# Gated recurrence: the scores of two levels in one stretch of TensorE tiles, with the odd level's queries copied aside by ScalarE

## The chip, the cores and the metric

One NeuronCore of a Trainium2 chip runs the whole program; nothing is shared with another core. The metric is the device time of one execution in microseconds, the median of several runs. The profile is one such execution, recorded by the hardware.

## The reference, cut to what matters

A two-layer encoder trunk is run on two batches (512 and 256 tokens, here 768 tokens side by side, width 1024). Layer 0 mixes tokens by a gated recurrence in both directions, layer 1 by windowed attention, and each layer has a feed-forward block ahead of its mixer and one behind. The change touches the recurrence alone:

```python
def gla_chunk_scan(q, k, v, logf):
    """q, k, logf: [B,T,H,K]; v: [B,T,H,V]. S_t = diag(f_t) S_{t-1} + k_t v_t^T, o_t = S_t^T q_t."""
    ...
        b = jnp.cumsum(fi.astype(F32), axis=1)
        o_inter = jnp.einsum('bchk,bhkv->bchv', qf * jnp.exp(b), S)
        ...
        A = jnp.einsum('bthk,btshk,bshk->bhts', qf, jnp.exp(rel), kf)
        o_intra = jnp.einsum('bhts,bshv->bthv', A, vf)
```

There are 8 heads of 128 channels. The scan runs once forward and once backward in time, and the two results are added.

## The kernel before, in words

**Where the recurrence stands.** The feed-forward block comes first. Then `hgrn` runs the heads one behind the other. For each head `hgrn_proj` makes queries, two forget gates and keys by projections (three matmuls in float32r for each product, lines 258 to 260), and `hgrn_scan` does the recurrence. While head h is scanned, the projection of head h+1 is fed in between in pieces: `weave` runs one step of the scan up to its `yield`, then some pieces of the projection, so that TensorE has work while VectorE and ScalarE prepare the next step. In head 3 the value projection of the second half is fed in as well (42 pieces in place of 18), in head 6 there are four pieces fewer, and in head 7 it is the projection of the output gate that is fed in.

**The levels.** Within a block of 128 tokens the scores are made by 7 levels of halving. At level l the tokens stand in runs of J = 2^l; a query of one run meets the keys of the run beside it. `q` and `k` hold, for both directions, values that are multiplied in place by the running products of gates (`totals`) after each level, so that they fit the next one. One level before is: ScalarE copies the keys of the level into `kop` in token order (line 702); TensorE makes the scores of 6 blocks in 12 matmuls of a 128x64 tile (`scan_scores`, line 675), reading the queries straight out of `q`; VectorE puts the result into the score matrix `A` (`put`: a copy at line 693 or a copy under a mask at line 696, two instructions a level); VectorE multiplies `q` (line 718, one instruction), `k` (line 722, one for each direction) and `totals` (line 724). At level 0 the scores of every token with itself are made as well, from the untouched queries `qs` and the sum of keys `kd`. Behind level 6 come the transposes (line 738), the chunk sums (line 746) and the output (line 770).

**What sets the order.** The program is written in this order, and a scheduler then lays out a fixed queue for each engine; an engine works through its queue in order, and waits between engines are semaphores. All three of TensorE, VectorE and ScalarE carry both the scan of head h and the projection of head h+1: on ScalarE the evictions of the projection (line 657), the weight casts (line 166) and the complement of the gates (line 662) stand between the key copies; on VectorE the weight remainders (line 167) and the gate arithmetic (lines 661, 663, 664) stand between the level's instructions.

Of the kernel before, what the change touches and what calls it, by code (L numbers as in the profile page):

```python
# [16 lines left out]
P = 128  # L17
# [5 lines left out]
T = TA + TB  # L23
# [3 lines left out]
LEVELS = 7  # L27
# [20 lines left out]
class Trunk:  # L48
# [559 lines left out]
            yield  # L608

    @staticmethod  # L610
    def weave(main, feed, pieces, steps=LEVELS + 1):
        used = 0
        for i, _ in enumerate(main):
            while used * steps < (i + 1) * pieces:
                used += 1
                next(feed, None)
# [53 lines left out]
    def scan_scores(self, lhs, rhs):  # L670
        ps = self.ps(NBLK * 64)
        for b in range(NBLK):
            for par in range(2):
                rows = slice(par * 64, (par + 1) * 64)
                self.nc.tensor.matmul(ps[rows, b * 64 : (b + 1) * 64], lhs(b)[:, rows], rhs(b, par), start=True, stop=True)  # L675
        return ps

    def hgrn_scan(self, hd, v):
        nc = self.nc
        h, qs, kd, f, q, k = (hd[n] for n in ("h", "qs", "kd", "f", "q", "k"))  # L680
        ka = self.big([P, 2, T])
        kop, A = ka[:, 0, :], ka[:, 1, :]
        totals = self.big([P, 2, T])
        blk = lambda t, b: t[:, b * P : (b + 1) * P]

        def put(level, ps):
            for par in range(2):
                rows = slice(par * 64, (par + 1) * 64)
                c = 1 - par if level == LEVELS - 1 else par
                dst = A.rearrange("p (b c j) -> p b c j", c=2, j=64)[rows, :, c, :]  # L690
                src = ps[rows, :].rearrange("p (b j) -> p b j", j=64)
                if level in (0, LEVELS - 1):
                    nc.vector.tensor_copy(dst, src)
                    continue
                m = self.masks[rows, level, c * 64 : (c + 1) * 64].unsqueeze(1).to_broadcast([64, NBLK, 64])
                nc.vector.copy_predicated(dst, m, src)

        tot, base = f, 0
        for l in range(LEVELS):
            c, J = T >> l, 1 << l  # L700
            kv = bass.AP(k.tensor, k.offset, [list(k.ap[0]), [2 * J, c // 2], [T + J, 2], [1, J]])
            nc.scalar.copy(kop.rearrange("p (b g j) -> p b g j", g=2, j=J), kv)

            def rhs(b, par):
                part = list(q.ap[0])
                if J == 64:
                    return bass.AP(q.tensor, q.offset + b * P + (0 if par else T + J), [part, [1, J]])
                at = q.offset + b * P + par * 64
                return bass.AP(q.tensor, at, [part, [2 * J, 64 // (2 * J)], [T + J, 2], [1, J]])

            put(l, self.scan_scores(lambda b: blk(kop, b), rhs))
            if l == 0:
                own = lambda b, par: qs[:, b * P + par * 64 : b * P + (par + 1) * 64]
                put(LEVELS, self.scan_scores(lambda b: blk(kd, b), own))
            part = [list(q.ap[0])]
            both = bass.AP(q.tensor, q.offset, part + [[T + J, 2], [2 * J, c // 2], [1, J]])
            t = bass.AP(tot.tensor, tot.offset + base + 1, [list(tot.ap[0]), [T - 1, 2], [2, c // 2], [0, J]])
            nc.vector.tensor_mul(both, both, t)
            for d in range(2):
                xv = self.halves(k, l, d, d)  # L720
                t = tot[:, 1 - d, base + 1 - d : base + c : 2].unsqueeze(2).to_broadcast([P, c // 2, J])
                nc.vector.tensor_mul(xv, xv, t)
            nbase = 0 if l == 0 else base + c
            nc.vector.tensor_mul(
                totals[:, :, nbase : nbase + c // 2], tot[:, :, base : base + c : 2], tot[:, :, base + 1 : base + c : 2]
            )
            tot, base = totals, nbase
            yield

        F, Bk = 1, 0  # L730
        order = ((0, 0), (0, 1), (0, 2), (0, 4), (1, 1), (1, 2), (1, 3), (1, 5))
        kT = self.big([P, 8, P])
        S = self.big([P, 8, P])
        for half in range(2):
            pt = self.ps()
            for i in range(4):
                d, b = order[half * 4 + i]
                nc.tensor.transpose(pt[:, i * P : (i + 1) * P], blk(k[:, d, :], b), self.ident)
            nc.scalar.copy(kT[:, half * 4 : half * 4 + 4, :], pt.rearrange("p (a b) -> p a b", a=4))
        vb = lambda b: v[b][:, h * P : (h + 1) * P]  # L740
        pds = []
        for half in range(2):
            pd = self.ps()
            for i in range(4):
                d, b = order[half * 4 + i]
                nc.tensor.matmul(pd[:, i * P : (i + 1) * P], kT[:, half * 4 + i, :], vb(b), start=True, stop=True)  # L746
            pds.append(pd)
        state = {}
        for d, steps in ((0, ((0, None), (1, 0), (2, 1), (4, None))), (1, ((3, None), (2, 3), (1, 2), (5, None)))):
            for b, prev in steps:  # L750
                i = order.index((d, b))
                ds = pds[d][:, (i % 4) * P : (i % 4 + 1) * P]
                if prev is None:
                    nc.scalar.copy(S[:, i, :], ds)
                else:
                    dec = totals[:, 1 - d, base + b : base + b + 1]
                    nc.vector.scalar_tensor_tensor(S[:, i, :], S[:, order.index((d, prev)), :], dec, ds, ALU.mult, ALU.add)
                state[(d, b)] = S[:, i, :]
        yield
        pos = [self.ps(n) for _, n in SEQS]  # L760
        for b in range(NBLK):
            s, i = (0, b) if b < 4 else (1, b - 4)
            o = pos[s][:, i * P : (i + 1) * P]
            terms = [(blk(A, b), vb(b))]
            if (0, b - 1) in state and b != 4:
                terms.append((blk(q[:, F, :], b), state[(0, b - 1)]))
            if (1, b + 1) in state and b != 3:
                terms.append((blk(q[:, Bk, :], b), state[(1, b + 1)]))
            for j, (l_, r_) in enumerate(terms):
                nc.tensor.matmul(o, l_, r_, start=(j == 0), stop=(j == len(terms) - 1))  # L770
        for s, (off, n) in enumerate(SEQS):
            nb = n // P
            sq = self.tmp(n)
            nc.scalar.square(sq, pos[s])
            for b in range(nb):
                nc.scalar.copy(vb(off // P + b), pos[s][:, b * P : (b + 1) * P])
            nc.vector.tensor_reduce(
                self.hss[:, h, off // P : off // P + nb], sq.rearrange("p (b j) -> p b j", b=nb), AX.X, ALU.add
            )
# [485 lines left out]
```

## Time and profile before

| What | Value |
|---|---|
| Time, median of 3 runs | 2799.03 us (2798.24 to 2800.07) |
| The profiled execution | 2799.1 us, its span 2797.3 us, the 1.8 us beside it being start and end |
| Instructions in the span | 42176 |
| Granted TensorE clock | 0.998 of full speed |
| The scan, first to last score matmul | 580.1 us to 921.2 us, 1536 matmul records on line 675 |
| Key copies of ScalarE, line 702 | 56, median 837 ns |

In the profile a TensorE time is that of the start of an operation and its modelled end, so matmuls that follow each other overlap in the list; the distance from one start to the next is what an operation costs. A score matmul in float32 appears as two records. The score group of one level is therefore 24 records, and two groups behind each other are one stretch.

### The profile page before, as it was taken

How to read it: one execution, taken by the hardware profiler on the slowest of the kernel's cores; microseconds unless marked ns; L12 is line 12 of the kernel's file. 1: busy time of each engine (PE TensorE's matmuls, PEld its weight loads, DVE VectorE, ACT ScalarE, POOL GpSimd, SP SyncE). 2: the span in 40 equal slices, each digit the busy share in tenths (PEclk: the TensorE clock that was granted, in tenths of full speed). 3: DMA queues.
4: the chain of work that ended last, by engine and by line, in shares of the span. 5: the costliest groups of instructions: out<-in, count | busy, mean ns of one | idle time of the engine just before them, and what ended most of it. 6: DMA issues, size and time to landing. Idle time of an engine off the chain costs nothing.

```text
span 2797.3 us, 42176 instructions
## 1 busy us (share of the span) xinstructions
PE 2768.5 (99%) x16129; PEld 2493.3 (89%) x16129; DVE 2168.3 (78%) x3750; ACT 1283.9 (46%) x2383; POOL 308.6 (11%) x312
## 2 busy tenths in 40 slices
PE   8999999999999999999999999999999999999998
PEld 8999999888888889999999999999876679999998
DVE  7788788578598658788878878887847768788877
ACT  7444444434344435444445544444546655444443
POOL 1111111000000001211111121111100001211110
PEclk9999999999999999999999999999999999999999
DMA  5554564311111322655444255544512113655443
GB/s 160 132 125 117 125 140 124 113 52 41 54 39 31 103 72 76 143 132 128 119 113 124 76 145 132 122 117 118 143 61 76 46 47 76 146 135 121 125 111 108
DMA packets 330106, 291.47 MB, mean 104 GB/s; under 512 B 11608, under 2 KB 257840, under 8 KB 329904
## 3 DMA queue, kind: packets, MB, share of 16 engines
q1 hardware_dynamic: 294064, 212.43, 25.4%
q0 software_dynamic: 31680, 62.93, 13.3%
q10 hardware_dynamic: 4160, 13.42, 1.4%
q8 instruction: 126, 2.06, 0.3%
q14 instruction: 76, 0.62, 0.1%
HBM read 216.39 MB, written 9.44 MB: 81 GB/s over the span
## 4 chain that ended last, share of the span: by engine, by line
PE 94%; DVE 4%; ACT 1%; issue 0%; DMA 0%; DVEq 0%; SPq 0%; ACTq 0%
PE ps L418 40%; PE ps L482 20%; PE ps L258 9%; PE ps L259 8%; PE ps L260 8%; PE ps L675 2%; PE ps L1139 1%; PE ps L1089 1%; PE ps L770 1%; PE ps L1129 1%; PE ps L320 1%; PE ps L746 1%; DVE w L200 0%; DVE big L264 0%; DVE w L167 0%
## 5 line engine op out<-in xcount | busy, mean ns | idle before, releaser
L418 PE MATMUL ps<-big,w 128*128 128x384 f32 x6720 | 1172.6, 334 | 1.2 <-ACT tA L435 1.2
L418 PEld LDWEIGHTS ps<-big,w 128*128 128x128 f32 x6720 | 1165.3, 188 | 6.8 <-ACT tA L435 4.8
L199 ACT CAST w<-wr 128x512 fp32r<-128x512 f32 x600 | 415.8, 707 | 687.8 <-DVE wr L213 355.3
L200 DVE TENSOR_TENSOR w<-wr,w 128x512 fp32r<-128x512 f32 (+1 forms) x520 | 449.0, 867 | 181.3 <-ACT w L199 171.9
L482 PE MATMUL ps<-w,big 128*128 128x512 f32 x2520 | 575.7, 389 | 0.9 <-DVE x L504 0.9
L482 PEld LDWEIGHTS ps<-w,big 128*128 128x128 f32 x2520 | 472.6, 188 | 98.9 <-ACT big L263 1.3
L504 DVE SCALAR_TENSOR_TENSOR x<-ps,x 128x512 f32<-128x512 f32 x468 | 303.9, 681 | 10.7 <-PE ps L260 10.0
L141 POOL DMA_DIRECT2D s<-wr x120 | 105.1, 876 | 1706.0 <-DMA wr<-in_ffn_w_dram 847.1
L258 PE MATMUL ps<-w,big 128*128 128x512 f32 x624 | 253.0, 405 | 0.3
L260 PE MATMUL ps<-w,big 128*128 128x512 f32 x624 | 244.4, 392 | 1.0 <-DVE big L327 1.0
L259 PE MATMUL ps<-w,big 128*128 128x512 f32 x624 | 244.1, 391 | 0.0
L258 PE MATMUL ps<-big,w 128*128 128x384 f32 (+2 forms) x640 | 221.6, 348 | 2.7 <-ACT big L263 1.6
L259 PE MATMUL ps<-big,w 128*128 128x384 f32 (+2 forms) x640 | 217.0, 339 | 0.7 <-DVE big L264 0.6
L260 PE MATMUL ps<-big,w 128*128 128x384 f32 (+2 forms) x640 | 215.8, 337 | 0.0
L263 ACT CAST big<-tA 128x384 fp32r<-128x384 f32 x296 | 148.0, 513 | 144.7 <-DVE tA L450 64.9
L264 DVE TENSOR_TENSOR big<-tA,big 128x384 fp32r<-128x384 f32 x296 | 179.0, 615 | 13.2 <-ACT big L263 12.2
L167 DVE TENSOR_TENSOR w<-wr,w 128x1024 fp32r<-128x1024 f32 x92 | 112.0, 1220 | 69.3 <-ACT w L166 63.5
L166 ACT CAST w<-wr 128x1024 fp32r<-128x1024 f32 x92 | 96.7, 1052 | 120.6 <-PE ps L259 101.1
L258 PEld LDWEIGHTS ps<-w,big 128*128 128x128 f32 x624 | 117.2, 188 | 30.1 <-issue 6.8
L200 POOL TENSOR_TENSOR w<-wr,w 128x512 fp32r<-128x512 f32 x80 | 123.0, 1537 | 171.6 <-ACT w L199 170.2
L260 PEld LDWEIGHTS ps<-w,big 128*128 128x128 f32 x624 | 117.1, 188 | 27.1 <-DVE big L327 1.7
L259 PEld LDWEIGHTS ps<-w,big 128*128 128x128 f32 x624 | 117.4, 188 | 21.5 <-issue 0.4
(160 smaller groups left out, 2960.5 us busy)
## 6 DMA issues: line engine op xcount, KB each, us to landing
wr<-in_ffn_w_dram SPq DMA_DIRECT2D x264, 512.0 KB, 3.9
s<-in_ffn_w_dram SPq DMA_DIRECT2D x120, 256.0 KB, 3.1
s<-wr POOLq DMA_DIRECT2D x120, 256.0 KB, 4.4
wr<-wr POOLq DMA_DIRECT2D x80, 256.0 KB, 3.7
wr<-in_hg_w_in_dram SPq DMA_DIRECT2D x40, 512.0 KB, 3.8
wr<-wr POOLq DMA_DIRECT2D x20, 512.0 KB, 4.6
spill<-x ACTq DMA_DIRECT2D x12, 512.0 KB, 2.7
x<-spill ACTq DMA_DIRECT2D x12, 512.0 KB, 3.3
```

Source lines behind the costliest of these rows:

```text
L141: self.nc.gpsimd.dma_start(out, src, accum_op=ALU.add)
L167: self.nc.vector.tensor_sub(lo, raw, hi.bitcast(F32))
L199: nc.scalar.copy(h, src)
L200: low = (eng or nc.vector).tensor_sub(l, src, h.bitcast(F32)).ins
L258: nc.tensor.matmul(out, a[0], b[0], start=first, stop=False)
L259: nc.tensor.matmul(out, a[0], b[1], start=False, stop=False)
L260: nc.tensor.matmul(out, a[1], b[0], start=False, stop=last)
L263: self.nc.scalar.copy(hi, src)
L264: self.nc.vector.tensor_sub(lo, src, hi.bitcast(F32))
L418: self.nc.tensor.matmul(ps, a[x], b[y], start=first and k == 0 and i == 0, stop=k == 3 and i == 2, skip_group_check=True,)
L482: nc.tensor.matmul(ps, a[x], w[y], start=name == chain and kp == 0 and q == 0, stop=kp == 1 and q == 2, skip_group_check=True,)
L504: self.nc.vector.scalar_tensor_tensor(x, ps, c, x, ALU.mult, ALU.add)
```

## The change

Two levels now share one step of the scan. Step by step: level 0 with the scores of every token with itself, as before; levels 1 and 2; levels 3 and 4; levels 5 and 6. `yield` stands only behind the even levels, and `weave` divides the projection pieces by 5 steps in place of 8.

In a step with levels l-1 and l (l even), the operands of the odd level are copied aside when it is their turn, its in-place multiplications are done, then the operands of the even level are copied, and only then both score groups are issued: the even level first, the odd one pinned right behind it. The odd level's queries would be overwritten by then, so ScalarE copies them into `qs` in token order (line 707), 24 copies more in all. Its keys go to `spare`, the even level's keys to `kd`, whose first contents are no longer needed (line 705).

```diff
-    def weave(main, feed, pieces, steps=LEVELS + 1):
+    def weave(main, feed, pieces, steps=LEVELS // 2 + 2):
...
-                self.nc.tensor.matmul(ps[rows, b * 64 : (b + 1) * 64], lhs(b)[:, rows], rhs(b, par), start=True, stop=True)
-        return ps
+                mm = self.nc.tensor.matmul(
+                    ps[rows, b * 64 : (b + 1) * 64], lhs(b)[:, rows], rhs(b, par), start=True, stop=True
+                )
+        return ps, mm.ins
...
-        kop, A = ka[:, 0, :], ka[:, 1, :]
+        spare, A = ka[:, 0, :], ka[:, 1, :]
...
+        def operands(l):
+            J = 1 << l
+            part, runs = list(q.ap[0]), [[2 * J, T // (2 * J)], [T + J, 2], [1, J]]
+            kop = kd if l and l % 2 == 0 else spare
+            view = lambda t: t.rearrange("p (b g j) -> p b g j", g=2, j=J)
+            nc.scalar.copy(view(kop), bass.AP(k.tensor, k.offset, [list(k.ap[0])] + runs))
+            if l % 2:
+                nc.scalar.copy(view(qs), bass.AP(q.tensor, q.offset, [part] + runs))
+
+            def rhs(b, par):
+                at = b * P + par * 64
+                if l % 2:
+                    return qs[:, at : at + 64]
...
+            return l, lambda b: blk(kop, b), rhs
+
+        own = lambda b, par: qs[:, b * P + par * 64 : b * P + (par + 1) * 64]
+        waiting = []
         tot, base = f, 0
         for l in range(LEVELS):
             c, J = T >> l, 1 << l
-            kv = bass.AP(k.tensor, k.offset, [list(k.ap[0]), [2 * J, c // 2], [T + J, 2], [1, J]])
-            nc.scalar.copy(kop.rearrange("p (b g j) -> p b g j", g=2, j=J), kv)
...
-            put(l, self.scan_scores(lambda b: blk(kop, b), rhs))
+            waiting.append(operands(l))
             if l == 0:
-                own = lambda b, par: qs[:, b * P + par * 64 : b * P + (par + 1) * 64]
-                put(LEVELS, self.scan_scores(lambda b: blk(kd, b), own))
+                waiting.append((LEVELS, lambda b: blk(kd, b), own))
+            if l % 2 == 0:
+                banks, last = [], None
+                for level, left, right in reversed(waiting) if l else waiting:
+                    with self.tc.issue_after(last) if last else nullcontext():
+                        ps, last = self.scan_scores(left, right)
+                    banks.append((level, ps))
+                for level, ps in banks:
+                    put(level, ps)
+                waiting = []
...
             tot, base = totals, nbase
-            yield
+            if l % 2 == 0:
+                yield
```

**TensorE, head 1, levels 1 and 2.** In these rows `ps_5622` (before) and `ps_5625` (now) are the bank of a projection piece of head 2, `big_5123` is `q` of head 1, `big_5121` holds `qs` and `kd`, `big_5553` or `big_5556` holds the key copies. Before:

```order
L258 MATMUL ps_5622<-big_4591,w_5213 128x512
L259 MATMUL ps_5622<-big_4591,w_5213 128x512
L260 MATMUL ps_5622<-big_4591,w_5214 128x512
L675 MATMUL ps_5630<-big_5123,big_5553 64x64 x12
L258 MATMUL ps_5622<-big_4592,w_5213 128x512
L259 MATMUL ps_5622<-big_4592,w_5213 128x512
L260 MATMUL ps_5622<-big_4592,w_5214 128x512
```

Now, at the step of levels 1 and 2:

```order
L258 MATMUL ps_5625<-big_4593,w_5213 128x512
L259 MATMUL ps_5625<-big_4593,w_5213 128x512
L260 MATMUL ps_5625<-big_4593,w_5214 128x512
L675 MATMUL ps_5645<-big_5123,big_5121 64x64 x12
L675 MATMUL ps_5658<-big_5121,big_5556 64x64 x12
L258 MATMUL ps_5625<-big_4594,w_5213 128x512
L259 MATMUL ps_5625<-big_4594,w_5213 128x512
L260 MATMUL ps_5625<-big_4594,w_5214 128x512
```

A group of one level between projection matmuls has become two groups with nothing between them. Over a head, the projection matmuls between the groups (each row of three is one product) stood before as 30, 12, 18, 18, 18, 24 and, behind level 6, 12 up to the transposes and 12 inside the last part; now they stand as 36, 36, 24, and 30 and 18 behind the group of levels 6 and 5.

**VectorE, head 1, from level 4 to level 6.** `big_5124` is `k`, `big_5123` is `q`, `big_5554` (now `big_5557`) is `totals`, `big_5553` (now `big_5556`) holds `A`; `w_5734` and `w_5718` are weight remainders, `big_5464` to `big_5468` the gates and queries of head 2. Before:

```order
L167 TENSOR_TENSOR w_5734<-wr_5217,w_5733 128x1024
L696 COPY_PREDICATED big_5553<-big_4691,ps_5748 64x6x64 x2
L718 TENSOR_TENSOR big_5123<-big_5123,big_5554 128x2x24x16
L722 TENSOR_TENSOR big_5124<-big_5124,big_5554 128x24x16
L724 TENSOR_TENSOR big_5554<-big_5554 128x2x24
L661 TENSOR_SCALAR big_5464<-big_5464,lb_buf 128x768
L663 TENSOR_TENSOR big_5465<-big_5463,big_5464 128x768
L722 TENSOR_TENSOR big_5124<-big_5124,big_5554 128x12x32 x2
L696 COPY_PREDICATED big_5553<-big_4691,ps_5787 64x6x64 x2
L718 TENSOR_TENSOR big_5123<-big_5123,big_5554 128x2x12x32
L724 TENSOR_TENSOR big_5554<-big_5554 128x2x12
L722 TENSOR_TENSOR big_5124<-big_5124,big_5554 128x6x64 x2
```

Now:

```order
L167 TENSOR_TENSOR w_5718<-wr_5217,w_5717 128x1024
L698 COPY_PREDICATED big_5556<-big_4691,ps_5731 64x6x64
L698 COPY_PREDICATED big_5556<-big_4691,ps_5744 64x6x64 x2
L739 TENSOR_TENSOR big_5123<-big_5123,big_5557 128x2x24x16
L661 TENSOR_SCALAR big_5467<-big_5467,lb_buf 128x768
L745 TENSOR_TENSOR big_5557<-big_5557 128x2x24
L743 TENSOR_TENSOR big_5124<-big_5124,big_5557 128x12x32
L739 TENSOR_TENSOR big_5123<-big_5123,big_5557 128x2x12x32
L743 TENSOR_TENSOR big_5124<-big_5124,big_5557 128x12x32
L745 TENSOR_TENSOR big_5557<-big_5557 128x2x12
L663 TENSOR_TENSOR big_5468<-big_5466,big_5467 128x768
L743 TENSOR_TENSOR big_5124<-big_5124,big_5557 128x6x64 x2
```

The masked copies of levels 4 and 3 (`ps_5731`, `ps_5744`) now stand ahead of the multiplications for level 5, the masked copies of the level just ahead of 6 have moved behind it, and the second half of `k` for level 6 (the second `128x12x32`) stands behind the multiplication of `q`.

**ScalarE, head 1, the same place.** Before:

```order
L657 ACTIVATE big_5464<-ps_5622 128x512
L702 COPY big_5553<-big_5124 128x768
L166 CAST w_5733<-wr_5217 128x1024
L657 ACTIVATE big_5464<-ps_5688 128x256
L702 COPY big_5553<-big_5124 128x768
L662 ACTIVATE big_5466<-big_5464 128x768
L657 ACTIVATE big_5464<-ps_5740 128x512
L702 COPY big_5553<-big_5124 128x768
```

Now:

```order
L657 ACTIVATE big_5467<-ps_5625 128x512
L705 COPY big_5121<-big_5124 128x768
L166 CAST w_5717<-wr_5217 128x1024
L657 ACTIVATE big_5467<-ps_5692 128x256
L705 COPY big_5556<-big_5124 128x768
L707 COPY big_5121<-big_5123 128x768
L662 ACTIVATE big_5469<-big_5467 128x768
L657 ACTIVATE big_5467<-ps_5765 128x512
L705 COPY big_5121<-big_5124 128x768
```

The row with `L707` is the new copy of level 5's queries; the last row is the key copy of level 6, for which the group of levels 6 and 5 waits.

More of the change, by code (lines that the diff above doesn't have):

```diff
@@ L696, in put @@
                 nc.vector.copy_predicated(dst, m, src)
+        def operands(l):
[10 more added lines that the diff above has]
+                    return qs[:, at : at + 64]
+                if J == 64:
+                    return bass.AP(q.tensor, q.offset + b * P + (0 if par else T + J), [part, [1, J]])
+                return bass.AP(q.tensor, q.offset + at, [part, [2 * J, 64 // (2 * J)], [T + J, 2], [1, J]])
+            return l, lambda b: blk(kop, b), rhs
+        own = lambda b, par: qs[:, b * P + par * 64 : b * P + (par + 1) * 64]
+        waiting = []
         tot, base = f, 0
@@ L700, in hgrn_scan @@
             c, J = T >> l, 1 << l
-            kv = bass.AP(k.tensor, k.offset, [list(k.ap[0]), [2 * J, c // 2], [T + J, 2], [1, J]])
[L702 to L709, printed above, removed]
-            put(l, self.scan_scores(lambda b: blk(kop, b), rhs))
-            if l == 0:
-                own = lambda b, par: qs[:, b * P + par * 64 : b * P + (par + 1) * 64]
-                put(LEVELS, self.scan_scores(lambda b: blk(kd, b), own))
+            waiting.append(operands(l))
+            if l == 0:
+                waiting.append((LEVELS, lambda b: blk(kd, b), own))
[8 more added lines that the diff above has]
+                waiting = []
             part = [list(q.ap[0])]
```

## The prediction

> **What bounds the kernel now.** I read the page first: busy times and the chain that ended last.
>
> ```profile
> PE 2768.5 (99%) x16129; PEld 2493.3 (89%) x16129; DVE 2168.3 (78%) x3750; ACT 1283.9 (46%) x2383; POOL 308.6 (11%) x312
> PE 94%; DVE 4%; ACT 1%; issue 0%; DMA 0%; DVEq 0%; SPq 0%; ACTq 0%
> ```
>
> TensorE bounds the whole: 99% busy, 94% of the chain. VectorE's 78% is a mean over stages, so I cut the scan into windows: head 1 from its first score group to the group of level 6, head 1 from there to head 2's first group, then all of heads 3 and 6.
>
> ```profile
> core 0: us, PE busy (x) PEld busy (x) DVE busy (x) ACT busy (x) POOL busy (x), PEclk, DMA share, GB/s
> 619.65:646.59 26.94, 26.94 (x290) 23.16 (x289) 25.22 (x41) 10.69 (x20) 0.00 (x0) 1.00 0.14 40
> 646.59:659.22 12.63, 12.63 (x101) 11.09 (x101) 10.06 (x19) 6.64 (x14) 0.00 (x0) 1.00 0.15 43
> 698.80:771.13 72.33, 72.28 (x534) 60.94 (x533) 40.72 (x63) 24.95 (x43) 0.00 (x0) 1.00 0.19 52
> 850.31:892.27 41.96, 39.74 (x391) 34.28 (x390) 35.97 (x60) 18.75 (x38) 0.00 (x0) 1.00 0.14 39
> ```
>
> This is the row that decides the case. Between the group of level 0 and that of level 6 VectorE is busy 25.22 of 26.94 us: two engines are bound at once, and whoever takes TensorE's work out of this stretch finds VectorE behind it. Head 3 is different (40.72 of 72.33 us). Head 6 already waits, 41.96 - 39.74 = 2.22 us. A head takes 26.94 + 12.63 = 39.57 us. TensorE's waits between 575 and 935 us, by releaser, are few:
>
> ```profile
> PE ps L675 <- ACT big L702: 3.1, 2, 1.7
> PE ps L675 <- ACT big L657: 0.7, 1, 0.7
> PE ps L675 <- DVE big L718: 0.2, 1, 0.2
> ```
>
> **The change: what it saves.** The timeline of TensorE around the pair of level 0 and around one lone group:
>
> ```profile
> 619.65 1.22 PE L675 MATMUL ps<-big,big 128*64 128x64 f32 x24
> 620.70 0.87 PE L675 MATMUL ps<-big 128*64 128x64 f32 x24
> 621.50 0.39 PE L258 MATMUL ps<-big,w 128*128 128x256 f32 x1
> 621.72 0.28 PE L259 MATMUL ps<-big,w 128*128 128x256 f32 x1
> 621.84 0.28 PE L260 MATMUL ps<-big,w 128*128 128x256 f32 x1
> ...
> 629.47 0.39 PE L260 MATMUL ps<-big,w 128*128 128x512 f32 x1
> 629.79 0.92 PE L675 MATMUL ps<-big,big 128*64 128x64 f32 x24
> 630.64 0.50 PE L258 MATMUL ps<-big,w 128*128 128x512 f32 x1
> 630.97 0.39 PE L259 MATMUL ps<-big,w 128*128 128x512 f32 x1
> 631.20 0.40 PE L260 MATMUL ps<-big,w 128*128 128x512 f32 x1
> ```
>
> Starts are what counts. From one 512-wide matmul to the next it is 0.23 us (630.97 to 631.20), from one 256-wide to the next 0.12 us. Into the group it takes 0.32 us, 0.09 more than 0.23; the lone group takes 0.85 us, the second of a pair 0.80 us; the first matmul behind holds the next up 0.33 us, 0.10 more (0.22 for 0.12 at the pair). So joining two stretches saves 0.09 + 0.05 + 0.10 = 0.24 us. Three are joined in each of 8 heads: 24 x 0.24 = 5.8 us. That is the whole gain; the matmuls themselves stay. Its bounds are 0, if the switch is paid between the two groups as well, and 5.8; I take 5.8, since the pair of level 0 shows 0.80 for its second group.
>
> [...]
>
> **What it costs: head 1 walked through.** Time runs from its first score group, at 619.65. TensorE has three pairs (0.09 + 0.85 + 0.80 + 0.10 = 1.84 each), with 36, 36 and 24 projection matmuls behind them: 24 x 0.12 + 12 x 0.23 = 5.64, again 5.64, and 24 x 0.23 = 5.52. That is 22.32 us to the group of levels 6 and 5. The same sum for the order before (a pair, five lone groups of 0.09 + 0.85 + 0.10 = 1.04, 48 wide and 72 narrow matmuls) gives 26.72, against 26.94 measured, so 0.22 are waits. VectorE's rows in that head, and the last two steps of the chain to a group:
>
> ```profile
> 620.92 1.14 DVE L693 COPY big<-ps 64x384 f32<-64x384 f32 x2
> ...
> 625.64 1.23 DVE L167 TENSOR_TENSOR w<-wr,w 128x1024 fp32r<-128x1024 f32 x1 [0.39 <-ACT w L166]
> ...
> 641.04 0.55 DVE L722 TENSOR_TENSOR big<-big,big 128x384 f32<-128x384 f32 x1
> ...
> 641.62 0.67 DVE L661 TENSOR_SCALAR big<-big,lb_buf 128x768 f32<-128x768 f32 x1
> 641.70 0.84 ACT L702 COPY big<-big 128x768 f32<-128x768 f32 x1 [4.25 <-DVE big L724]
> ...
> 642.33 0.96 DVE L663 TENSOR_TENSOR big<-big,big 128x768 f32<-128x768 f32 x1
> 642.67 0.92 PE L675 MATMUL ps<-big,big 128*64 128x64 f32 x24
> 643.21 1.02 DVE L722 TENSOR_TENSOR big<-big,big 128x384 f32<-128x384 f32 x2
> 644.26 1.21 DVE L696 COPY_PREDICATED big<-big,ps 64x384 f32<-64x384 uint8 x2
> 645.48 0.96 DVE L718 TENSOR_TENSOR big<-big,big 128x768 f32<-128x768 f32 x1
> ```
>
> From 620.92 to the end of level 5's `q` at 646.44, with a gap of 0.39, VectorE puts away seven score groups and multiplies for six levels. In the queue now, ahead of the key copy of level 6, stand the same instructions but for two: the masked copies of level 5 (1.21) and line 663 (642.33 to 643.21, 0.88). They end at 646.44 - 0.39 - 1.21 - 0.88 = 643.96. Then ScalarE's key copy follows 0.11 us behind VectorE (641.04 + 0.55 = 641.59 to 641.70), takes 0.84, and TensorE starts 0.13 later (642.54 to 642.67): 1.08 together, so the group starts at 645.04, 25.39 us in. TensorE was ready at 22.32 and waits 3.07 us in all. Most falls ahead of the last pair, where `q` of level 5 stands between the two halves of `k`, and line 661 ahead of both, while the key copy waits for the second half.
>
> Behind that group TensorE does what it did, 12.63 us, and a second group (0.80), six products of the projection more up to the transposes (4.26 in place of 2.76) and six matmuls more ahead of the output (1.38): 16.31. The head takes 25.39 + 16.31 = 41.70 us, 2.13 more than 39.57. As a check: 3.07 of waits, less 3 x 0.24 saved, less the 0.22 that it waited before.
>
> The 24 copies of odd queries cost ScalarE about 20 us, by the row of the key copies, which read in the same pattern (median of the three numbers):
>
> ```profile
> L702 ACT COPY big<-big x56: 822/837/1213, 578.9 to 917.7; 128x768 f32<-128x768 f32 x56
> ```
>
> ScalarE has room (10.69 busy of 26.94). VectorE may overwrite `q` only behind such a copy, 0.11 + 0.84 + 0.03, about 1.0 us; meanwhile it multiplies `k`, 1.02 us, or for level 5 lines 661 and 743, 0.67 + 0.55. So I put it at nothing; without that cover it is 1.0 us a copy, 24 us, and one that takes 1.21 shows 0.37.
>
> **The other heads.** The pairs of level 0 of heads 4 and 5 in the chain of waits:
>
> ```profile
> 771.20 1.85 PE ps L675 x48
> ...
> 810.80 1.85 PE ps L675 x48
> ```
>
> Heads 0, 1, 2, 4 and 5 have the period of head 1 (39.60 here): 5 x 2.1 = 10.5. In head 4 a table load stands on ScalarE ahead of the eviction that precedes a key copy:
>
> ```profile
> L657 ACT ACT_TABLE_LOAD  x2: 1283/1283/1283, 557.5 to 783.3; - x2
> ```
>
> It was hidden; now the key copy of level 4 stands behind it with TensorE waiting, so between 0 and 1.28 us shows; I take 0.9. Head 3 has VectorE idle for 31.6 us and only saves: 3 x 0.24, -0.7. In head 6 only 13 projection matmuls stand between the pairs of levels 2 and 4: TensorE is ready after 1.84 + 13 x 0.23 = 4.83 us. The chain there is group (0.97), four masked copies (2.42), `q` (0.96), half of `k` (0.55), an eviction and a key copy on ScalarE (0.11 + 0.58 + 0.84), `k` (1.03), handover and copy (1.08): 8.54, a wait of 3.7. The rest of its chain I put at 1.3, under half of head 1's 3.07, since VectorE catches up in the long wait; less 0.7 and the 2.22 of before, +2.1. Head 7 has VectorE work of the output gate in the place of the next head's: I put it at 2.1 like its neighbours. Sum: 10.5 + 0.9 - 0.7 + 2.1 + 2.1 = 14.9. On the profiled execution's 2799.1 us, 0.07 above the median, that gives 2814.0. No DMA is moved past a wait that matters: weights were never what TensorE waited for here, and the queues of SyncE and GpSimd keep their order.
>
> **Rivals.**
> - *TensorE stays the bound* (the other side). If VectorE is through 3.0 us sooner per head than my walk, no wait arises and the 5.8 remain: 2793.3. For it: before, TensorE hardly waited. Against: 25.22 us of VectorE's work in 26.94, of which 22.3 remain. Chance 0.06.
> - *A draw*: waits of about 0.9 a head (0.72 saved, 0.22 that go) eat the saving, VectorE 2.1 us sooner: 2799.1. Chance 0.05.
> - *The joined stretch saves nothing*, since the second group holds TensorE as long as a switch: 14.9 + 5.8, 2819.8. The pair of level 0 speaks against. Chance 0.08.
> - *The query copies lose their cover*: half of 24 us shows, 2826.0. For it: the three engines take turns twice per pair. Chance 0.06.
> - *The wait slows the clock.* Granted clock is 1.00 in every window above, but the longest wait is 1.7 us. If head 6's 3.7 us drops TensorE to half rate for as long again, 1.9 us more, 2815.9. Chance 0.10. [...]
>
> **How the numbers follow.** The forecast has 0.65: 2814.0. Its own bounds: if handover and copy (1.08) are hidden in all 8 heads, 8.6 less, 2805; if three query copies a head show 0.37, 8.9 more, 2823. This range holds most of the forecast, the clock and the case without saving, about 0.8. A measurement of this kernel can tell about 0.2% (5.6 us) from no change. Faster by more: 0.06; within: 0.05; slower by more: 0.89.
>
> **What would show it.** Right: a head of 41 to 42 us; TensorE idle 2 to 3 us ahead of the group of levels 6 and 5, released by ScalarE's key copy; VectorE without gaps from the first put to there; head 3 shorter by under 1 us; head 6 with a wait of 3 to 5 us. Wrong: heads below 39.57, or waits that VectorE ends directly at the odd query copies.

## The result, and the profile after

The changed kernel takes 2815.04 us (median of 6 runs, 2813.87 to 2815.95); the kernel before, timed beside it, 2799.55 us (6 runs, 2798.24 to 2803.3). The ratio is 1.0053, 95% interval [1.0042, 1.0064]: 15.5 us slower. The profiled execution took 2813.97 us, 14.9 more than that of before (2799.1).

The page after: busy time of each engine, and the shares of the chain that ended last.

```profile
PE 2763.8 (98%) x16129; PEld 2495.1 (89%) x16129; DVE 2165.3 (77%) x3750; ACT 1301.8 (46%) x2407; POOL 306.4 (11%) x312
...
PE 89%; DVE 7%; ACT 2%; issue 1%; DMA 1%; DVEq 0%; ACTq 0%; SPq 0%
```

TensorE has less to do (2763.8 us after 2768.5), and the kernel is slower all the same. VectorE's part of the chain rises from 4% to 7%, TensorE's falls from 94% to 89%. What TensorE waits for in the scan (575 to 955 us), by releaser: total us, times, longest.

```profile
PE ps L675 <- ACT big L705: 21.1, 13, 4.3
PE ps L768 <- ACT big L761: 1.4, 3, 0.9
PE ps L675 <- DVE big L739: 0.2, 1, 0.2
```

Before, the key copies released two waits of 3.1 us together; now they release 13 of 21.1 us. The three waits on line 768, the chunk sums, are new too and small beside them. The windows of head 1 from its first score group to the group of levels 6 and 5, and from there to head 2, then all of heads 0, 3 and 6:

```profile
core 0: us, PE busy (x) PEld busy (x) DVE busy (x) ACT busy (x) POOL busy (x), PEclk, DMA share, GB/s
622.69:647.58 24.89, 22.39 (x242) 19.43 (x241) 23.62 (x40) 12.87 (x22) 0.00 (x0) 1.00 0.15 43
647.58:663.76 16.18, 16.18 (x148) 14.66 (x149) 11.16 (x21) 6.66 (x14) 0.00 (x0) 1.00 0.11 33
580.75:622.69 41.94, 40.01 (x389) 35.53 (x389) 34.87 (x59) 18.77 (x30) 0.00 (x0) 0.96 0.13 39
704.85:776.25 71.40, 71.11 (x533) 61.01 (x532) 39.99 (x63) 27.30 (x46) 0.00 (x0) 1.00 0.19 53
859.27:903.90 44.63, 39.90 (x389) 34.92 (x388) 35.63 (x60) 21.18 (x41) 0.00 (x0) 0.96 0.13 37
```

Head 1 takes 24.89 + 16.18 = 41.07 us in place of 39.57. In its first part TensorE works 22.39 us and VectorE 23.62 of 24.89: the engine that fills the stretch has changed. Head 3, where VectorE has room, became shorter (71.40 after 72.33). In heads 0 and 6 the granted clock is 0.96.

The timeline of TensorE in head 1 shows where the time lies:

```profile
630.03 0.39 PE L260 MATMUL ps<-big,w 128*128 128x512 f32 x1
630.35 1.62 PE L675 MATMUL ps<-big,big 128*64 128x64 f32 x48
631.90 0.50 PE L258 MATMUL ps<-big,w 128*128 128x512 f32 x1
632.24 0.39 PE L259 MATMUL ps<-big,w 128*128 128x512 f32 x1
...
638.14 1.62 PE L675 MATMUL ps<-big,big 128*64 128x64 f32 x48 [0.35 <-ACT big L705]
...
647.58 1.62 PE L675 MATMUL ps<-big,big 128*64 128x64 f32 x48 [2.15 <-ACT big L705]
```

The pair of levels 2 and 1 is free of waits, that of levels 4 and 3 waits 0.35 us, that of levels 6 and 5 waits 2.15, each time for the even level's keys. The timeline of VectorE up to that group, with ScalarE's key copy as the last row:

```profile
641.16 1.82 DVE L698 COPY_PREDICATED big<-big,ps 64x384 f32<-64x384 uint8 x3
642.99 0.96 DVE L739 TENSOR_TENSOR big<-big,big 128x768 f32<-128x768 f32 x1
643.87 0.67 DVE L661 TENSOR_SCALAR big<-big,lb_buf 128x768 f32<-128x768 f32 x1
...
644.76 0.56 DVE L743 TENSOR_TENSOR big<-big,big 128x384 f32<-128x384 f32 x1
645.24 0.95 DVE L739 TENSOR_TENSOR big<-big,big 128x768 f32<-128x768 f32 x1
646.11 0.55 DVE L743 TENSOR_TENSOR big<-big,big 128x384 f32<-128x384 f32 x1
...
646.70 0.83 ACT L705 COPY big<-big 128x768 f32<-128x768 f32 x1 [0.60 <-DVE big L743]
```

VectorE has no gap there. The masked copies of levels 4 and 3 (four instructions; the first starts at 639.45, the row has the other three) stand ahead of `q` for level 5 and of both halves of `k` for level 6, which the next pair needs; the second half of `k` for level 6 ends at 646.66, the copy at 647.53, and TensorE starts at 647.58.

### The profile page after: what moved, and what is told of

Its sections match the earlier page's. It is cut to its first block, busy times and chain, and to the rows that moved or that the text cites. A ratio compares the mean times of both kernels' runs of the same rounds, so it can differ in the third digit from the quotient of the medians.

```text
span 2812.2 us, 42186 instructions
## 1 busy us (share of the span) xinstructions
PE 2763.8 (98%) x16129; PEld 2495.1 (89%) x16129; DVE 2165.3 (77%) x3750; ACT 1301.8 (46%) x2407; POOL 306.4 (11%) x312
## 4 chain that ended last, share of the span: by engine, by line
PE 89%; DVE 7%; ACT 2%; issue 1%; DMA 1%; DVEq 0%; ACTq 0%; SPq 0%
PE ps L418 40%; PE ps L482 20%; PE ps L258 8%; PE ps L259 7%; PE ps L260 7%; PE ps L675 1%; DVE big L698 1%; PE ps L1161 1%; PE ps L1111 1%; DVE big L739 1%; PE ps L792 1%; PE ps L1151 1%; DVE big L743 1%; DVE w L167 1%; PE ps L320 1%
```

## The experiments

**Theory.** Joining the levels is a gain for TensorE by itself. The loss is one of order in VectorE's queue: the masked copies of both levels (line 698) and the multiplications of two levels follow each pair, so the next pair's keys come too late for what TensorE has left to do. **Rival.** The 24 query copies of ScalarE (line 707) cost the time, by themselves or because VectorE must wait for them before it overwrites `q`. The chip ran six kernels, each the changed one with an edit.

**1. Without the query copies** (the odd levels' queries are then never copied; the matmuls read what stands in `qs`).

```diff
-            if l % 2:
-                nc.scalar.copy(view(qs), bass.AP(q.tensor, q.offset, [part] + runs))
```

> The changed kernel without ScalarE's 24 copies of the odd levels' queries; the odd levels then read what stands in qs, so this part of the computation is left out. Queue theory (VectorE's queue between the pairs is longer than TensorE's filler; the copies are covered by the multiplication of k): 2812 to 2815 us, since VectorE has no gap at these copies. Copy theory (the handover VectorE to ScalarE to VectorE at each copy is what TensorE waits for in the end, 24 x 1.0 us): about 2791 us.

Measured: 2818.89 us, ratio to before 1.0063 [1.0048, 1.0078]. No gain, where the rival had 24 us. The waits in the scan are longer than with the copies, 24.9 us in place of 21.1, a difference of 3.8 that neither theory had (the intervals of the two ratios overlap, so that this kernel is slower than the changed one is read from the waits, not shown by the times). Part of its time is the clock: four of its waits are followed by a stretch of TensorE's clock at 0.50 to 0.65, two in the changed kernel, at 0.50 (see the last section). The timeline of TensorE for the last pair of head 0 and the last two of head 1, then of VectorE ahead of the last:

```profile
605.38 2.42 PE L675 MATMUL ps<-big,big 128*64 128x64 f32 x48 [2.54 <-ACT big L705]
...
638.95 1.62 PE L675 MATMUL ps<-big,big 128*64 128x64 f32 x48 [0.81 <-ACT big L705]
648.81 1.62 PE L675 MATMUL ps<-big,big 128*64 128x64 f32 x48 [2.54 <-ACT big L705]
```

```profile
643.54 0.96 DVE L736 TENSOR_TENSOR big<-big,big 128x768 f32<-128x768 f32 x1
644.41 0.68 DVE L661 TENSOR_SCALAR big<-big,lb_buf 128x768 f32<-128x768 f32 x1
...
645.13 0.96 DVE L663 TENSOR_TENSOR big<-big,big 128x768 f32<-128x768 f32 x1
646.00 0.95 DVE L736 TENSOR_TENSOR big<-big,big 128x768 f32<-128x768 f32 x1
646.87 1.02 DVE L740 TENSOR_TENSOR big<-big,big 128x384 f32<-128x384 f32 x2
```

Lines 736 and 740 are here what 739 and 743 were. With nothing to wait for, the scheduler lays VectorE's queue differently: line 663, a gate of the next head, and all of `q` stand ahead of both halves of `k`, and the key copy waits for the second half. In the changed kernel line 663 stands behind it. So this run also changed an order: by itself it is no clean price of the copies, and the next run and VectorE's own waits (further down) have to bear it out.

**2. The copies kept, one level a step.** The 24 copies and the new places of the operands stay, but each level's scores are issued in a step of their own, as before.

```diff
-    def weave(main, feed, pieces, steps=LEVELS // 2 + 2):
+    def weave(main, feed, pieces, steps=LEVELS + 1):
...
-            if l % 2 == 0:
+            if True:
                 banks, last = [], None
...
-            if l % 2 == 0:
-                yield
+            yield
```

> The changed kernel with one level a step again (a yield behind each level, eight steps for the projection pieces, each score group issued at once), but with the 24 query copies and the operands in spare and kd kept. Queue theory: the waits ahead of the pairs go and so does the saving of the joined stretches; 2799 to 2802 us, as before. Copy theory: the copies are still there, so 2810 us or more.

Measured: 2799.34 us, ratio 0.9994 [0.9985, 1.0004], no difference from before. The waits of TensorE in the scan:

```profile
PE ps L675 <- ACT big L705: 1.9, 2, 1.7
PE ps L675 <- ACT big L707: 1.5, 3, 0.7
```

All 24 query copies are there and cost nothing that can be measured: three waits now end on them, 1.5 us, but the 3.4 us of both rows are no more than the 4.0 of before. What costs is that the two levels stand together.

**3. Without the masked copies of levels 1 to 4** (these scores are made and never put away).

```diff
-                    put(level, ps)
+                    if level not in (1, 2, 3, 4):
+                        put(level, ps)
```

> The changed kernel without the masked copies of levels 1 to 4 (their scores are made but not put into the score matrix). VectorE has 8 instructions of 0.6 us less per head, 4.8 us, all ahead of the group of levels 6 and 5. Queue theory: the waits of 0.35 and 2.15 us per head and the 4.3 us of head 6 go, and the joined stretches show what they save (24 x 0.33 = 8 us): 2790 to 2794 us. Copy theory: the chain of handovers stays, 2810 us or more.

Measured: 2793.59 us, ratio 0.9972 [0.9961, 0.9983]. Waits of TensorE in the scan, and the window of head 1:

```profile
PE ps L675 <- ACT big L705: 3.1, 3, 1.7
```

```profile
620.49:658.94 38.45, 38.45 (x391) 34.06 (x392) 29.98 (x51) 19.77 (x37) 0.00 (x0) 1.00 0.15 42
```

With eight masked copies fewer a head VectorE keeps up, the waits are back to the 3.1 us that stood there before, and the joined kernel is faster than before. This shows two things: the wait is VectorE's, and joining does save time (38.45 for 39.57 us a head).

**4. More of the projection ahead of the last pair.** TensorE gets other work for the time in which it waits; VectorE's work is what it was.

```diff
-    def weave(main, feed, pieces, steps=LEVELS // 2 + 2):
+    def weave(main, feed, pieces, by=(4, 8, 14, 16, 18)):
...
-            while used * steps < (i + 1) * pieces:
+            while used * by[-1] < by[i] * pieces:
```

> The changed kernel with the projection pieces dealt out 4, 8, 14, 16, 18 (of 18) behind the five steps in place of equal fifths, so that two more pieces (2.7 us) stand ahead of the group of levels 6 and 5 and two fewer behind it. Queue theory: the wait of 2.15 us there is covered in every steady head, those of 0.35 us stay: about 2815 - 5 x 2.1 - 4 = 2800 us, and 2797 if head 6 loses its long wait too. If the pieces taken from behind the last pair were needed there (ahead of the transposes and the output), the wait moves there and the time stays at 2812 or more.

Measured: 2797.61 us, ratio 0.9988 [0.9979, 0.9997]. TensorE's timeline for the last two pairs of head 1:

```profile
634.77 1.62 PE L675 MATMUL ps<-big,big 128*64 128x64 f32 x48 [0.35 <-ACT big L705]
644.86 1.62 PE L675 MATMUL ps<-big,big 128*64 128x64 f32 x48
```

The wait of 2.15 us is gone with nothing taken from VectorE; that of 0.35, ahead of the pair that got no more work, stays. The scan's waits fall from 21.1 to 7.6 us.

**5. The masked copies one step later.** Nothing is left out here; only the place of these copies in VectorE's queue moves, behind the multiplications that the next pair needs.

```diff
-        waiting = []
+        waiting, held = [], []
...
-                for level, ps in banks:
+                for level, ps in held:
                     put(level, ps)
-                waiting = []
+                held, waiting = banks, []
...
+        for level, ps in held:
+            put(level, ps)
```

> The changed kernel with the copies and masked copies into the score matrix issued one step later, behind the next pair's scores in the program, so that 2.4 us of VectorE's work per pair stands behind what TensorE waits for and one pair's copies fall behind the group of levels 6 and 5, where VectorE has 3.5 us without work. The output is unchanged. Queue theory: 2.15 of the 2.5 us of waits per steady head go, 7 heads, and head 6's long wait shrinks: 2797 to 2801 us. If the work only moves inside the same queue, or the longer held PSUM banks make TensorE wait, 2808 us or more.

Measured: 2793.74 us, ratio 0.9978 [0.9969, 0.9988], better than expected: the key copies release 4.2 us of waits in place of 21.1, and no drop of the clock shows in the scan: its granted clock in head 1 is 1.00, and all its pairs take about 1.55 us, where the one behind the drop in head 6 of the changed kernel takes 2.76. VectorE ahead of the last pair of head 1, with ScalarE's key copy:

```profile
637.76 0.93 DVE L739 TENSOR_TENSOR big<-big,big 128x768 f32<-128x768 f32 x1
638.62 1.01 DVE L743 TENSOR_TENSOR big<-big,big 128x384 f32<-128x384 f32 x2
...
639.72 0.83 ACT L705 COPY big<-big 128x768 f32<-128x768 f32 x1 [2.37 <-DVE big L743]
639.74 1.85 DVE L698 COPY_PREDICATED big<-big,ps 64x384 f32<-64x384 uint8 x3
```

The window of head 1 from its first score group to that of levels 6 and 5:

```profile
619.04:640.60 21.56, 21.56 (x238) 18.84 (x237) 20.78 (x36) 11.94 (x20) 0.00 (x0) 1.00 0.17 50
```

Three of the four masked copies of levels 4 and 3 stand behind `k` instead of ahead of `q`. Line 661 (0.67), which stood ahead of `k` in the changed kernel, now starts at 643.51, so the scheduler moved more than the edit did. The key copy ends at 640.55, and the group starts at 640.60, 21.56 us into the head. The changed kernel needs 24.89: 2.50 of the difference are its waits, and 0.69 are three 512-wide matmuls that stand behind the group here. It is close: TensorE does not wait, but the copy comes no earlier than it is wanted. The expectation had left waits of 0.35 us in each head.

**6. Both of the last two edits together.**

> The last two edits together: pieces dealt out 4, 8, 14, 16, 18 and the copies into the score matrix a step later. Queue theory: with both, VectorE's chain is short enough and TensorE's filler long enough that the 7.6 us of waits left in the fourth run go but for the first (1.7): 2791 to 2794 us, and the 24 x 0.33 us of the joined stretches show against the kernel before. If other waits take their place, 2797 us or more.

Measured: 2792.6 us, ratio 0.9973 [0.9962, 0.9983]. Waits of TensorE in the scan:

```profile
PE ps L675 <- ACT big L705: 2.7, 3, 1.7
```

This beats both kernels with nothing left out: the one before by an interval that doesn't reach 1, by 7.9 us between the medians, the changed one by 22.4 (these two were not timed side by side). It and the fifth run can't be told apart by their intervals.

## Why the prediction was right, and where it was off

**What bounds it** was right: two engines were bound at once, and TensorE, relieved, waits for VectorE through ScalarE's key copy. Runs 3, 4 and 5 remove the wait in three ways: less work for VectorE, other work for TensorE, and another order. Four of the rivals fall: that TensorE stays the bound, that the waits only draw level, that the joined stretch saves nothing, and that the query copies lose their cover. The first of them describes runs 3, 5 and 6, where VectorE is in time: 2793.3 was its price, 2792.6 to 2793.7 were measured. That they meet so closely is in part luck: the price is 5.8 below the time before, and the three runs are 6.7 to 7.9 below the kernel timed beside them (2800.45 and 2800.96).

**The saving of a join was too small** in my sum (0.24 us each, 5.8 for 24). By the rows above the way into the pair takes 630.35 - 630.03 - 0.23 = 0.09, the pair 1.55, the way out 632.24 - 631.90 - 0.23 = 0.11, together 1.75; two lone groups of before are 2 x 1.04 = 2.08. That is 0.33 a join, 24 x 0.33 = 8 us. The second group of a pair takes 0.70, not the 0.80 that I read from level 0. Whole heads give a little more. Head 3 became 72.33 - 71.40 = 0.93 shorter, but TensorE waits 0.05 of it before and 0.29 now; without these it is 72.28 - 71.11 = 1.17, 0.39 for each of its three joins. Head 1 of run 3, where TensorE never waits, is 39.57 - 38.45 = 1.12 shorter, 0.37 each.

**The wait of a steady head** was forecast at 3.07 us and is 0.35 + 2.15 = 2.50. `k` is ready 23.97 us into the head (forecast 24.31), and handover and copy take 647.58 - 646.66 = 0.92 (forecast 1.08). Behind the group it is 16.18 (forecast 16.31). So the head is 1.5 us longer, not 2.1: the term was 0.6 too large, in heads 1, 2 and 5. The 0.13 us that I took for the last handover was none: the group at 642.67 shows no wait, TensorE was busy up to it; where it does wait, now, the handover is 647.58 - 647.53 = 0.05.

**One reading of the walk was wrong** and did little harm. I put the 0.22 us between the sum of 26.72 and the measured 26.94 down as waits, but the same row has TensorE busy for 26.94 of 26.94. What was missing is the first group of a head: 620.70 - 619.65 = 1.05, where I had 0.85. For the changed head, this 0.20 and the second groups of two pairs, 0.10 too long each, cancel: TensorE was put ready at 22.32 and works 22.39.

**The query copies at no cost** was right. The waits of VectorE in the scan of the changed kernel show all that they cost it, total, times and longest:

```profile
DVE big L739 <- ACT big L707: 0.7, 2, 0.5
```

That row is of multiplications of `q`: two of them wait for a query copy, 22 of 24 copies are covered. Run 2 has all 24 and no loss.

**Head 4, the table load.** Its last two pairs wait 1.44 and 1.89 us; ScalarE's table load stands ahead of the eviction and the key copy (791.91) for which the first of them waits:

```profile
790.13 1.28 ACT L657 ACT_TABLE_LOAD   x1
...
792.79 1.62 PE L675 MATMUL ps<-big,big 128*64 128x64 f32 x48 [1.44 <-ACT big L705]
...
801.97 1.62 PE L675 MATMUL ps<-big,big 128*64 128x64 f32 x48 [1.89 <-ACT big L705]
```

Together 3.33, 0.83 above the 2.50 of a steady head; 0.9 was forecast.

**The clock** is the rival that came true beside the forecast, and was not in its sum. Its half rate stands in the trace of before (granted clock 0.50 from 17.00 to 20.00 us, outside the scan); that a wait of 3.7 us would bring it, and for as long again, was my assumption, which no trace of before showed. TensorE's timeline at the start of head 0 and ahead of the second last pair of head 6:

```profile
580.75 1.23 PE L675 MATMUL ps<-big,big 128*64 128x64 f32 x24 [1.74 <-ACT big L705]
581.80 1.38 PE L675 MATMUL ps<-big 128*64 128x64 f32 x24
583.11 0.58 PE L258 MATMUL ps<-big,w 128*128 128x256 f32 x1
...
585.20 0.36 PE L258 MATMUL ps<-big,w 128*128 128x256 f32 x1
...
876.06 2.83 PE L675 MATMUL ps<-big,big 128*64 128x64 f32 x48 [4.33 <-ACT big L705]
878.82 0.41 PE L258 MATMUL ps<-big,w 128*128 128x256 f32 x1
```

In head 6 the wait is 4.33 us (forecast 3.7), and the pair behind it takes 2.76 us in place of 1.55, at a granted clock of 0.50: 1.2 us, where the rival had 1.9. The head's other waits are 44.63 - 39.90 - 4.33 = 0.40 us, where I had 1.3. The head takes 44.63 us, 2.7 longer than before, forecast 2.1. In head 0 the clock drops to 0.50 (582.00 to 585.20 us) behind the first wait, 1.74 us, which before had too, at a clock of 1.00. The second group takes 583.11 - 581.80 = 1.31 in place of 0.80, and the nine narrow matmuls behind it 585.20 - 583.11 = 2.09 in place of 0.22 + 8 x 0.12 = 1.18: 1.4 us. This head is 41.94 - 39.57 = 2.37 longer, forecast 2.1.

**The sum.** The scan grew by 13.0 us where 14.9 were forecast: heads 0, 1, 2, 4 and 5 at 2.4, 1.5, 1.5, 2.3 and 1.5, head 3 at -0.9, head 6 at 2.7, head 7 at 2.0 (each from its first score group, to the last products in head 7). The other 1.9 us lie in unchanged code, 0.7 ahead of the scan and 1.3 behind it in this one execution. In the eight traces the start of the scan moves by 2.3 us and the stretch behind it by 3.4, so I take it for the variation of runs; that was not shown. The total was met because terms that were off on both sides, and this remainder, cancelled; that 2815.04 lies so near 2814.0 is luck, and the mechanism is what was right.

## What to carry to other kernels

Joining work on the busiest engine also joins what hangs on it: two score groups at once mean two puts at once in the queue of the next engine, and where that engine is nearly as full (here 25.22 of 26.94 us), the order there can decide: 2815.04 us with the masked copies ahead of the keys, 2793.74 with most of them behind. Look for the result that the next group waits for, and put only what it needs ahead of it; what merely stores a result can come a step later. And a wait that is removed lets the scheduler choose another order, so an experiment that takes something away should be read in the new order, not in the old one less one instruction.

## What the runs showed of the hardware

The granted clock dropped to 0.50 behind a wait of 1.74 us, less than half of the 3.7 that my rival had. The windows of the changed kernel: behind a wait of 1.74 us, behind one of 2.15, and behind one of 4.33.

```profile
582.00:585.20 3.20, 3.20 (x34) 3.08 (x30) 3.01 (x5) 0.92 (x1) 0.00 (x0) 0.50 0.02 5
647.50:651.00 3.50, 3.42 (x63) 3.35 (x64) 3.44 (x8) 0.03 (x1) 0.00 (x0) 1.00 0.02 5
876.06:878.90 2.84, 2.84 (x49) 2.72 (x49) 2.17 (x4) 0.00 (x0) 0.00 (x0) 0.50 0.00 0
```

The wait of 1.74 us at the start of head 0 stands in all eight traces, and only in the changed kernel was it followed by a drop, to 0.50. In the first run, without the query copies, a wait of 2.54 us was followed by a stretch at 0.61 in head 0 and by one at 1.00 in head 1:

```profile
605.30:608.00 2.70, 2.62 (x49) 2.51 (x50) 2.30 (x5) 0.02 (x1) 0.00 (x0) 0.61 0.00 0
648.80:652.00 3.20, 3.19 (x61) 3.12 (x62) 3.13 (x6) 0.00 (x0) 0.00 (x0) 1.00 0.02 5
```

Of the four waits of 2.54 to 2.57 us in heads 0, 1, 2 and 5 of that run three were followed by a drop (a clock of 0.61, 0.60 and 0.65 over the 2.5 to 2.7 us behind them) and the one in head 1 was not, and its wait of 3.40 us was followed by one too (0.50 from 883.00 to 885.50 us). A drop cost 1.2 to 1.4 us in the changed kernel and about 1.5 in run 1 (head 0: the pair takes 2.34 in place of 1.55, the seven narrow matmuls behind it 1.65 in place of 0.94). Why a drop comes behind some waits of one length and not behind others was not shown.
